# First MLP product of a two-layer decoder trunk: token operand's high and low part streamed as one 512-column product

## Chip, cores and metric

The kernel runs on one core of one Trainium2 chip. The metric is the device time of one execution in microseconds (us), as the median of the runs. Instruction starts and durations come from one profiled execution.

## What is computed

The reference is a trunk of two layers on 256 tokens of width 2048, all in float32. The part that matters here is the MLP of each layer, with 8192 hidden columns:

```python
m = rmsnorm(h, pre_ff_norm)
y = jnp.square(jax.nn.relu(m @ w_ff1)) @ w_ff2
h = h + rmsnorm(y, post_ff_norm)
```

Ahead of it stand an input projection, sparse attention with a top-k indexer, retention and an output projection. Behind it stands a gated per-layer embedding. Every large product is made from float32 weights that are read once from device memory.

## The kernel before

**Split products.** Each float32 operand is cut into a high part (rounded to the type float32r) and a low part (what the rounding left). A product is the sum of three: high times high, high times low, low times high. TensorE thus makes three passes for each tile of 128 rows of the contraction (a K-tile, 16 of them in the width of 2048).

**Weight stream.** `prep` (L260) loads two K-tiles of 512 weight columns (a half, 512 KB) by a DMA on SP's queue into one of 3 buffers `raw`. ScalarE writes the high part `whi` (L271) and VectorE the low part `wlo` (L272), each into one of 7 buffers. A `Unit` holds two halves (four K-tiles) and its matmuls. The loop over units (L958 on) calls `prep_to` ahead of the unit's matmuls, and the unit's `after` behind them.

**Token-major products.** `a_units` (L275): the tokens are the stationary operand, 512 weight columns stream past (L291, L292, L293), and each of two token tiles has its own PSUM bank. The second MLP product `ff2` (L856) is made so, in pieces of 8 K-tiles. Its result is added into `Y` by VectorE (L867, L865 for the first piece).

**Transposed products.** `b_units` (L302) is used for the first MLP product alone: 128 weight columns are stationary and all 256 tokens stream past. For each of four column blocks `f` and each K-tile `k` of a unit it issues `whi` past the tokens' high part (L321), `whi` past their low part (L324) and `wlo` past their high part (L325), 256 columns each. Blocks `f` 0 and 1 share a bank, and so do 2 and 3, so that a chunk of 512 hidden columns takes two banks of the pool `ps_mm`. There are 2 layers of 8 pieces, with 2 chunks of 4 units in each.

**Behind a chunk.** `after` in `ff1` (L830) runs for each bank: Relu from the bank (L837) and Square into the high part of the hidden operand `fT` (L838) on ScalarE, then the same square in float32 (L840) and the low part (L841) on VectorE.

**Order.** Units go `ff1(0)`, `ff1(1)`, `ff2(0)`, `ff1(2)`, `ff2(1)` and so on to `ff2(7)`, so the hidden operand of a piece is used about a piece later. A scheduler orders each engine's instructions, and on each engine they are issued in that order.

**Buffers.** K-major operands of 2048 rows are `TSet`s (L214): four slots of the pool `H` (8 slots, 8 KB per partition each), two for high parts and two for low ones. Attention's operands, the hidden operand and half of the embedding product (`e1`, L816) come from `H` too. PSUM has 4 banks for large products (`ps_mm`) and 4 for transposes and small products (`ps_ax`).

Of the kernel before, what the change touches and what calls it, by code (L numbers as in the profile page):

```python
# [36 lines left out]
# columns of the constants: a part for retention alone, and a part that stays on chip  # L37
# [5 lines left out]
class Unit:  # L43
    """Up to four K-tiles of weights, and the matmuls that use them."""
# [12 lines left out]
def trunk(ctx: ExitStack, tc: tile.TileContext, x, p, positions, w_in, w_out, w_ff1, w_ff2, w_ple, w_ple_gate,  # L57
# [6 lines left out]
    hp = ctx.enter_context(tc.tile_pool(name="hp", bufs=8))  # L64
# [6 lines left out]
    # what the weights' split waits behind  # L71
# [53 lines left out]
    def tables():  # L125
        posf = small(NT, tag="posf", bufs=1)
        V.tensor_copy(posf, posi)
        ang = t2()[:, :NT * NROT]
        for t in range(NT):
            V.tensor_scalar(ang[:, t * NROT:(t + 1) * NROT], K[:, C_INV:C_INV + NROT], posf[:, t:t + 1], None, op0=OP.mult)  # L130
        # 2 pi in parts of 8 bits, so that a part times a count of 15 bits is exact in float32
        parts = _two_pi_parts()
        MAGIC = 1.5 * 2.0 ** 23
        BIG = MAGIC * 2.0 ** 14
        r = ang
        for _ in range(2):
            n = t2()[:, :NT * NROT]
            V.tensor_scalar(n, r, 0.15915494309189535, None, op0=OP.mult)
            hi = t2()[:, :NT * NROT]
            V.tensor_scalar(hi, n, BIG, BIG, op0=OP.add, op1=OP.subtract)  # L140
            lo = t2()[:, :NT * NROT]
            V.tensor_sub(lo, n, hi)
            V.tensor_scalar(lo, lo, MAGIC, MAGIC, op0=OP.add, op1=OP.subtract)
            for c in parts:
                for q in (hi, lo):
                    V.scalar_tensor_tensor(r, q, -c, r, op0=OP.mult, op1=OP.add)
        lim = 3.1415925
        V.tensor_scalar(r, r, lim, -lim, op0=OP.min, op1=OP.max)
        s1 = t2()[:, :NT * NROT]
        A.activation(s1, r, AF.Sin)  # L150
        V.tensor_tensor(sinT.rearrange("q t n -> q t n"), s1.rearrange("q (t n) -> q t n", t=NT),
                        K[:, None, C_SGN:C_SGN + NROT].to_broadcast([P, NT, NROT]), op=OP.mult)
        a1 = t2()[:, :NT * NROT]
        V.scalar_tensor_tensor(a1, r, -1.0, r, op0=OP.mult, op1=OP.max)
        V.tensor_scalar(a1, a1, -1.0, 1.5707963267948966, op0=OP.mult, op1=OP.add)
        A.activation(cosT.rearrange("q t n -> q (t n)"), a1, AF.Sin)

# [1 line left out]
    def root(v, n):  # L159
        """1/sqrt(v) on [P, n]: exponent guess, three Newton steps y (3 - v y^2) with the halves taken out beforehand."""  # L160
# [21 lines left out]
    class RowStat:  # L182
        """1/rms of rows from sums of squares that come in four parts; the first three are summed before the last is known."""
# [30 lines left out]
    class TSet:  # L214
        """K-major halves (hi, lo) of a [tokens, 2048] operand."""

        def __init__(self):
            self.hi = [None, None]
            self.lo = [None, None]

        def half(self, i):
            if self.hi[i] is None:
                self.hi[i] = hslot()
                self.lo[i] = hslot()
            return self.hi[i], self.lo[i]

# [3 lines left out]
    def after_first(first, m):  # L230
        """Keep m behind the matmul that opened its bank: the opening clears the whole bank's flags."""
        behind(m, first)
        return first or m

    def split_bank(ts, kt0, t, bank, gain=None):
        """bank [P, 4, 128] of K-tiles kt0.. for token tile t -> hi/lo."""
# [15 lines left out]
    def to_kmajor(ts, src, t, n, gain=None):  # L252
        """src: function col0 -> [P, 128] token-major block."""
# [6 lines left out]
    def prep(u, k):  # L260
        """K-tiles k, k+1 of the unit: load, and split into float32r parts."""
# [13 lines left out]
    def a_units(w, kts, cols, ts, after, kt_w0=0, ps=ps_mm):  # L275
        """Token-major product: psum[t] [128 tok, n] over K-tiles kts of ts; after(t, psum)."""
# [25 lines left out]
    def b_units(w, cols, ts, after):  # L302
        """Transposed product: psum [128 out cols, 256 tok], two column tiles per bank."""
        acc = []
        res = []
        for j in range(0, KT, 4):
            def mm(u, t, k0, j=j):
                if k0:
                    return
                opened = None  # L310
                if not acc:
                    acc.extend([ps_mm(), ps_mm()])
                for f in range(4):
                    o = acc[f // 2][:, (f % 2) * S:(f % 2 + 1) * S]
                    for k in range(4):
                        whi, wlo = u.halves[k // HALF]
                        ahi, alo = ts().get(j + k)
                        fc = slice(f * P, (f + 1) * P)
                        first = j + k == 0 and f % 2 == 0
                        last = j + k == KT - 1  # L320
                        m = T.matmul(o, whi[:, k % HALF, fc], ahi, start=first, stop=False, skip_group_check=True)  # L321
                        if j + k == 0:
                            opened = after_first(opened if f % 2 else None, m)
                        T.matmul(o, whi[:, k % HALF, fc], alo, start=False, stop=False, skip_group_check=True)  # L324
                        T.matmul(o, wlo[:, k % HALF, fc], ahi, start=False, stop=last, skip_group_check=True)  # L325
            fin = None
            if j + 4 >= KT:
                def fin(t):
                    for b in range(2):
                        after(b, acc[b])  # L330
# [6 lines left out]
    def soon(f, t):  # L337
        """In front of the side work, token tile 0 before 1."""
        side.insert(t, f)

# [1 line left out]
    def first_act():  # L342
        """K-major operand of a layer's input projection, from h; the norm's scale comes later."""
        st["aT"] = TSet()
# [12 lines left out]
    def rope(z, t, heads, width, kind):  # L357
        """In place on z [P, heads*width]."""
# [18 lines left out]
    def layer(l):  # L377
# [5 lines left out]
        def skew(n=2):  # L383
            """The last n units so far: first token tile first, for its successors' sake."""
# [16 lines left out]
        def load_zc():  # L401
# [4 lines left out]
            # block-diagonal pairs of retention states  # L406
            L["R"] = zc[:, Z_R:].rearrange("q (a e n) -> q a e n", a=4, e=2)

# [27 lines left out]
        def tr4(z, dst, j0, t):  # L436
            """Four [P, 128] blocks of z -> dst[:, j0:j0+4, tok], after the next unit."""
# [36 lines left out]
        def sc(t):  # L474
            # token tile 0 has 128 keys in row 2, tile 1 has 256 in row 0
            return L["score"][:, 2, 0:128] if t == 0 else L["score"][:, 0, :]

        def logits(t, hs):
            # heads of one parity: their operands lie in the same rows of the array
# [20 lines left out]
        def topk(t, rnd):  # L500
# [5 lines left out]
            if rnd == 3:  # L506
                nk = (t + 1) * P
                # not selected -> NEG, and not causal -> NEG
# [48 lines left out]
        def att_b(t, h0, n):  # L557
            """P -> P^T: [s, heads, q] per key block."""
# [8 lines left out]
            # [s, block, head, q]  # L567
            L["pt", t, h0] = pt.rearrange("q (b n) -> q b n", b=nb)

        def att_c(h0):  # L570
            """out^T [hd, heads, q] for 4 heads, both token tiles -> K-major halves."""
# [63 lines left out]
        def ret_inner(t, e):  # L635
            """Heads of parity e: decayed scores, transposed: [key, head, query]."""
# [62 lines left out]
        # first the chunk that needs the least: the rotary tables take their time  # L699
# [27 lines left out]
        def settle(t, ts, gain, step, sq):  # L727
            """Residual and next operand; both token tiles' first K-tiles come first."""
# [17 lines left out]
        def normed(src, t, n, i, ts, gain, step, eps=(EPS, EPS)):  # L746
            """Block n, the i-th to come, of a product that is normed and added to h."""
# [16 lines left out]
        def after_mix(n):  # L764
            def f(t, ps):
                if t == 0 and n == 0:
                    alloc_y()
                if t == 0 and n == 3:
                    L["mT"] = TSet()
# [3 lines left out]
        def mlp_scale():  # L773
            """The MLP runs on rows of h that are not normed: with v their mean square + eps, its result is v times too
            large, which the norm after it takes out if its eps is v^2 times larger."""
# [34 lines left out]
        def after_e(n):  # L810
            def f(t, ps):
                if n % 2 == 0 and t == 0:
                    if n == 0:
                        L["e"] = {0: sp.tile([P, NT, 2, 512], F32, name=nm("e0"), tag="zc", bufs=1)}
                    else:
                        L["e"][1] = hp.tile([P, NT, 2, 512], F32, name=nm("e1"), tag="H")  # L816
# [7 lines left out]
        NP = DFF // 1024  # L824

        def ff1(pc):
            res = []

            def after(c):
                def f(b, ps):  # L830
# [6 lines left out]
                    A.activation(u, ps, AF.Relu)  # L837
                    A.activation(hi[:, k:k + 2, :], u3, AF.Square)  # L838
                    sq = t2()
                    V.tensor_mul(sq, u, u)  # L840
                    V.tensor_sub(lo[:, k:k + 2, :], sq.rearrange("q (f n) -> q f n", f=2), hi[:, k:k + 2, :].bitcast(F32))  # L841
                return f
            for c in range(2):
                c0 = pc * 1024 + c * 512
                res += b_units(f1, (c0, c0 + 512), lambda: L["mT"], after(c))
# [113 lines left out]
    while i < len(units):  # L959
        # units of which the first token tile's products come first, or one unit  # L960
# [9 lines left out]
        if len(step) > 1:  # L970
            spare = HALVES - 2 * len(step)
            prep_to(end + spare)
            for t in range(NT):
# [7 lines left out]
                # as buffers come free, but not in the way of what was just started  # L981
# [36 lines left out]
def _constants():  # L1018
    """Tables that depend on shapes alone."""
# [50 lines left out]
```

## Time and profile before

| what | value |
|---|---|
| runs, us | 2425.32, 2423.05, 2427.38; median 2425.32 |
| profiled execution, span from first to last instruction | 2422.3 us; the profile lists no other time of that execution |
| TensorE matmuls (PE) | 2394.2 us busy, 99% of the span, 13737 |
| TensorE weight loads (PEld) | 2103.6 us, 87% |
| VectorE (DVE) | 1439.9 us, 59% |
| ScalarE (ACT) | 1171.1 us, 48% |
| granted TensorE clock, mean | 0.998 of full speed |
| moved from device memory | 439.91 MB, 182 GB/s over the span |

Matmuls are pipelined: the recorded duration of one is longer than the time until the next starts. What a stream of them costs is read from the distances of their starts, not from their durations. The queues of ScalarE and VectorE are followed in order: an instruction that waits holds all that stand behind it on that engine.

### The profile page before, as it was taken

What the parts mean: (1) busy time and instruction counts of PE and PEld (TensorE: products, weight loads), DVE (VectorE), ACT (ScalarE), POOL (GpSimd) and SP (SyncE); (2) the same over time, 40 slices, a digit from 0 to 9 for tenths busy, and PEclk for the clock granted to TensorE, in tenths of its full rate; (3) what the DMA queues carried; (4) which work ended last, traced back from release to release, by engine and by line L of the source; (5) the groups of instructions that cost most, each with busy time, mean ns of one, the idle gap of its engine ahead of it and who ended that gap; (6) DMA issues with size and microseconds to landing.
All of it is one profiled execution on the core that took longest, in us unless ns stands there. A gap on an engine that the chain in (4) does not pass through costs nothing.

```text
span 2422.3 us, 34917 instructions
## 1 busy us (share of the span) xinstructions
PE 2394.2 (99%) x13737; PEld 2103.6 (87%) x13737; DVE 1439.9 (59%) x2176; ACT 1171.1 (48%) x1598; POOL 2.1 (0%) x6
## 2 busy tenths in 40 slices
PE   8999999999999999999999999999999999999998
PEld 6888888989989989988888888899889989989886
DVE  6676756545555555557576767575455555555575
ACT  6545546544344334445475555474444344344453
POOL 0000000000000000000000000000000000000000
PEclk9999999999999999999999999999999999999999
DMA  7655465665666566565565555655665565665654
GB/s 240 181 166 154 144 199 174 189 193 186 181 191 193 184 191 190 182 202 183 184 201 175 165 148 159 203 169 186 193 191 183 184 198 183 186 195 184 200 187 135
DMA packets 235347, 444.27 MB, mean 183 GB/s; under 512 B 18528, under 2 KB 23472, under 8 KB 235184
## 3 DMA queue, kind: packets, MB, share of 16 engines
q1 hardware_dynamic: 233952, 441.24, 59.2%
q8 instruction: 107, 1.75, 0.3%
q10 hardware_dynamic: 1232, 0.82, 0.1%
q14 instruction: 56, 0.46, 0.1%
HBM read 439.91 MB, written 2.10 MB: 182 GB/s over the span
## 4 chain that ended last, share of the span: by engine, by line
PE 88%; DVE 4%; ACT 3%; DMA 3%; issue 1%; ACTq 0%; SPq 0%; DVEq 0%
PE mm L291 18%; PE mm L292 18%; PE mm L293 18%; PE mm L324 10%; PE mm L325 10%; PE mm L321 10%; DMA raw<-in_w_in 2%; DVE wlo L272 2%; ACT whi L271 1%; PE ax L484 1%; ACT t L248 1%; DVE h L722 1%; PE ax L256 0%; PE ax L537 0%; PE ax L579 0%
## 5 line engine op out<-in xcount | busy, mean ns | idle before, releaser
L272 DVE TENSOR_TENSOR wlo<-raw,whi 128x1024 fp32r<-128x1024 f32 (+1 forms) x824 | 994.2, 1217 | 841.1 <-ACT whi L271 834.4
L271 ACT ACTIVATE whi<-raw 128x1024 fp32r<-128x1024 f32 (+1 forms) x824 | 858.6, 1054 | 1067.4 <-PE mm L293 613.1
L291 PE MATMUL mm<-whi,H 128*128 128x512 f32 (+1 forms) x2240 | 875.2, 391 | 0.1
L292 PE MATMUL mm<-wlo,H 128*128 128x512 f32 (+1 forms) x2240 | 868.9, 388 | 0.4 <-DVE wlo L272 0.4
L293 PE MATMUL mm<-whi,H 128*128 128x512 f32 (+1 forms) x2240 | 868.1, 388 | 0.0
L324 PE MATMUL mm<-H,whi 128*128 128x256 f32 x2048 | 579.7, 283 | 0.7 <-DVE H L250 0.7
L321 PE MATMUL mm<-H,whi 128*128 128x256 f32 x2048 | 579.6, 283 | 0.3 <-ACT H L249 0.3
L325 PE MATMUL mm<-H,wlo 128*128 128x256 f32 x2048 | 579.5, 283 | 0.0
L291 PEld LDWEIGHTS mm<-whi,H 128*128 128x128 f32 x2240 | 420.9, 188 | 87.6 <-issue 2.7
L293 PEld LDWEIGHTS mm<-whi,H 128*128 128x128 f32 x2240 | 420.7, 188 | 85.7 <-DVE H L250 0.7
L292 PEld LDWEIGHTS mm<-wlo,H 128*128 128x128 f32 x2240 | 420.9, 188 | 83.1 <-DVE wlo L272 0.7
L324 PEld LDWEIGHTS mm<-H,whi 128*128 128x128 f32 x2048 | 393.1, 192 | 1.6 <-DVE H L250 1.1
L321 PEld LDWEIGHTS mm<-H,whi 128*128 128x128 f32 x2048 | 393.0, 192 | 1.7 <-ACT H L249 1.2
L325 PEld LDWEIGHTS mm<-H,wlo 128*128 128x128 f32 x2048 | 393.1, 192 | 0.0
L867 DVE TENSOR_TENSOR Y<-mm,Y 128x512 f32<-128x512 f32 x112 | 72.0, 683 | 3.0 <-PE mm L293 3.0
L837 ACT ACTIVATE t<-mm 128x512 f32<-128x512 f32 x64 | 37.7, 589 | 49.5 <-PE mm L325 49.5
L840 DVE TENSOR_TENSOR t<-t 128x512 f32<-128x512 f32 x64 | 44.0, 688 | 25.5 <-ACT t L837 25.5
L248 ACT ACTIVATE t<-ax,gK 128x128 f32<-128x128 f32 x160 | 46.8, 401 | 7.1 <-PE ax L256 6.7
L841 DVE TENSOR_TENSOR H<-t,H 128x512 fp32r<-128x512 f32 x64 | 44.1, 689 | 3.7 <-DVE t L840 0.5
L838 ACT ACTIVATE H<-t 128x512 fp32r<-128x512 f32 x64 | 40.1, 627 | 1.0
L250 DVE TENSOR_TENSOR H<-t,H 128x512 fp32r<-128x512 f32 x40 | 27.6, 690 | 15.7 <-ACT H L249 15.6
L256 PE MATMUL ax<-K,h 128*128 128x128 f32 x192 | 31.0, 299 | 5.7 <-DMA h<-in_x 3.6
(129 smaller groups left out, 828.5 us busy)
## 6 DMA issues: line engine op xcount, KB each, us to landing
raw<-in_w_ff SPq DMA_DIRECT2D x512, 512.0 KB, 4.0
raw<-in_w_in SPq DMA_DIRECT2D x160, 512.0 KB, 3.6
raw<-in_w_out SPq DMA_DIRECT2D x64, 512.0 KB, 4.5
raw<-in_w_ple_gate SPq DMA_DIRECT2D x64, 512.0 KB, 4.8
raw<-in_w_in SPq DMA_DIRECT2D x16, 256.0 KB, 3.1
raw<-in_w_ple SPq DMA_DIRECT2D x8, 512.0 KB, 4.7
h<-in_x SPq DMA_DIRECT2D x4, 512.0 KB, 5.7
gB<-in_post_mix_norm SPq DMA_DIRECT2D x8, 256.0 KB, 3.8
```

Source lines behind the costliest of these rows:

```text
L248: A.activation(u3[:, j, :], b3[:, j, :], AF.Copy, scale=gK[:, gain + kt0 + j:gain + kt0 + j + 1])
L271: behind(A.activation(hi[:, :, :u.n], raw[:, :, :u.n], AF.Copy), ha)
L272: behind(V.tensor_sub(lo[:, :, :u.n], raw[:, :, :u.n], hi[:, :, :u.n].bitcast(F32)), hv)
L291: T.matmul(o, ahi[:, tok], whi[:, k % HALF, :n], start=first, stop=False)
L292: T.matmul(o, ahi[:, tok], wlo[:, k % HALF, :n], start=False, stop=False)
L293: T.matmul(o, alo[:, tok], whi[:, k % HALF, :n], start=False, stop=last)
L321: m = T.matmul(o, whi[:, k % HALF, fc], ahi, start=first, stop=False, skip_group_check=True)
L324: T.matmul(o, whi[:, k % HALF, fc], alo, start=False, stop=False, skip_group_check=True)
L325: T.matmul(o, wlo[:, k % HALF, fc], ahi, start=False, stop=last, skip_group_check=True)
L840: V.tensor_mul(sq, u, u)
L841: V.tensor_sub(lo[:, k:k + 2, :], sq.rearrange("q (f n) -> q f n", f=2), hi[:, k:k + 2, :].bitcast(F32))
L867: V.tensor_add(L["Y"][:, t, sl], ps, L["Y"][:, t, sl])
```

## The change

The pair of high and low part of a K-tile becomes one moving operand of two runs of 256 columns, and the corrections get a half of the bank of their own:

- `TSet(paired=True)` takes one buffer `[128, 2, 8, 256]` for each 8 K-tiles from a new pool `xp` (tag `X`, 2 buffers of 16 KB), in which high and low parts lie side by side. The layer's input operand `aT` and the MLP's operand `mT` are paired now. `hp` has 4 slots in place of 8. `e1` comes from `X`.
- `b_units` issues two matmuls for each `f` and `k`: `whi` past both parts, 512 columns (L329), and `wlo` past the high part, 256 columns, into the bank's second half (L331). Each `f` has a bank of its own, four for a chunk; the first chunk of a piece takes the four of `ps_mm`, the second the four of `ps_ax`.
- Behind a chunk, for two banks each: ScalarE copies the second half of each bank (L845), VectorE adds the first half to it (L846), and ScalarE makes Relu (L847), Square (L848) and the high part (L849) from chip memory; VectorE makes the low part (L850). The separate square on VectorE is gone.

```diff
-    hp = ctx.enter_context(tc.tile_pool(name="hp", bufs=8))
+    hp = ctx.enter_context(tc.tile_pool(name="hp", bufs=4))
+    xp = ctx.enter_context(tc.tile_pool(name="xp", bufs=2))
...
         def half(self, i):
             if self.hi[i] is None:
-                self.hi[i] = hslot()
-                self.lo[i] = hslot()
+                if self.paired:
+                    self.both[i] = xp.tile([P, 2, 8, S], F32R, name=nm("X"), tag="X")
+                    self.hi[i], self.lo[i] = self.both[i][:, 0], self.both[i][:, 1]
+                else:
+                    self.hi[i] = hslot()
+                    self.lo[i] = hslot()
             return self.hi[i], self.lo[i]
+
+        def pair(self, kt):
+
+            return self.both[kt // 8][:, :, kt % 8, :]
...
-                opened = None
                 if not acc:
-                    acc.extend([ps_mm(), ps_mm()])
+                    acc.extend(ps() for _ in range(4))
                 for f in range(4):
-                    o = acc[f // 2][:, (f % 2) * S:(f % 2 + 1) * S]
+                    fc = slice(f * P, (f + 1) * P)
                     for k in range(4):
                         whi, wlo = u.halves[k // HALF]
-                        ahi, alo = ts().get(j + k)
-                        fc = slice(f * P, (f + 1) * P)
-                        first = j + k == 0 and f % 2 == 0
-                        last = j + k == KT - 1
-                        m = T.matmul(o, whi[:, k % HALF, fc], ahi, start=first, stop=False, skip_group_check=True)
-                        if j + k == 0:
-                            opened = after_first(opened if f % 2 else None, m)
-                        T.matmul(o, whi[:, k % HALF, fc], alo, start=False, stop=False, skip_group_check=True)
-                        T.matmul(o, wlo[:, k % HALF, fc], ahi, start=False, stop=last, skip_group_check=True)
+                        both = ts().pair(j + k)
+                        T.matmul(acc[f].rearrange("q (e n) -> q e n", e=2), whi[:, k % HALF, fc], both, start=(j + k == 0), stop=False,
+                                 skip_group_check=True)
+                        T.matmul(acc[f][:, S:], wlo[:, k % HALF, fc], both[:, 0, :], start=False, stop=(j + k == KT - 1),
+                                 skip_group_check=True)
...
-                        after(b, acc[b])
+                        after(b, acc[2 * b:2 * b + 2])
...
-                    A.activation(u, ps, AF.Relu)
-                    A.activation(hi[:, k:k + 2, :], u3, AF.Square)
-                    sq = t2()
-                    V.tensor_mul(sq, u, u)
-                    V.tensor_sub(lo[:, k:k + 2, :], sq.rearrange("q (f n) -> q f n", f=2), hi[:, k:k + 2, :].bitcast(F32))
+                    for f in range(2):
+                        A.activation(u3[:, f], ps[f][:, S:], AF.Copy)
+                        V.tensor_add(u3[:, f], ps[f][:, :S], u3[:, f])
+                    A.activation(u, u, AF.Relu)
+                    A.activation(u, u, AF.Square)
+                    A.activation(hi[:, k:k + 2, :], u3, AF.Copy)
+                    V.tensor_sub(lo[:, k:k + 2, :], u3, hi[:, k:k + 2, :].bitcast(F32))
...
-                res += b_units(f1, (c0, c0 + 512), lambda: L["mT"], after(c))
+                res += b_units(f1, (c0, c0 + 512), lambda: L["mT"], after(c), (ps_mm, ps_ax)[c])
```

Two places show how instructions move. The first is TensorE within a unit of `ff1`, before; `H_3440` and `H_3441` are high and low part of the tokens, and `mm_4222` is a bank.

```order
L321 MATMUL mm_4222<-H_3440,whi_4046 128x256
L324 MATMUL mm_4222<-H_3441,whi_4046 128x256
L325 MATMUL mm_4222<-H_3440,wlo_4047 128x256
L321 MATMUL mm_4222<-H_3440,whi_4052 128x256
L324 MATMUL mm_4222<-H_3441,whi_4052 128x256
L325 MATMUL mm_4222<-H_3440,wlo_4053 128x256
```

The same place now; `X_3441` holds both parts, and `mm_4109` and `mm_4110` are the banks of blocks 0 and 1.

```order
L329 MATMUL mm_4109<-X_3441,whi_3959 128x512
L331 MATMUL mm_4109<-X_3441,wlo_3960 128x256
L329 MATMUL mm_4109<-X_3441,whi_3965 128x512
L331 MATMUL mm_4109<-X_3441,wlo_3966 128x256
...
L329 MATMUL mm_4110<-X_3441,whi_3959 128x512
L331 MATMUL mm_4110<-X_3441,wlo_3960 128x256
```

Three matmuls of 256 columns become one of 512 and one of 256, with the same weights in the same order.

The second place is ScalarE behind the second chunk of piece 1, before: Relu and Square of two banks among the weight splits (`whi`).

```order
L271 ACTIVATE whi_4722<-raw_4720 128x1024
L837 ACTIVATE t_949_4708<-mm_4478 128x512
L838 ACTIVATE H_4452<-t_949_4708 128x512
L271 ACTIVATE whi_4728<-raw_4726 128x1024
L837 ACTIVATE t_951_4714<-mm_4479 128x512
L271 ACTIVATE whi_4760<-raw_4758 128x1024
L838 ACTIVATE H_4452<-t_951_4714 128x512
```

The same place now.

```order
L282 ACTIVATE whi_4497<-raw_4495 128x1024
L845 ACTIVATE t_947_4477<-ax_4309 128x256
L845 ACTIVATE t_947_4477<-ax_4310 128x256
L847 ACTIVATE t_947_4477<-t_947_4477 128x512
L845 ACTIVATE t_948_4486<-ax_4311 128x256
L848 ACTIVATE t_947_4477<-t_947_4477 128x512
L282 ACTIVATE whi_4503<-raw_4501 128x1024
L849 ACTIVATE H_4277<-t_947_4477 128x512
L845 ACTIVATE t_948_4486<-ax_4312 128x256
L282 ACTIVATE whi_4535<-raw_4533 128x1024
L847 ACTIVATE t_948_4486<-t_948_4486 128x512
L282 ACTIVATE whi_4541<-raw_4539 128x1024
```

Four instructions of ScalarE become ten (the last Square and the last high part follow below these rows), and three weight splits stand among them where two stood. Outside the MLP the order on every engine is the same as before, and SP's queue of loads is the same throughout.

## Rows read from the trace of the kernel before

**Rows 1.** Page: busy time by engine; TensorE's granted clock in 40 slices.

```profile
PE 2394.2 (99%) x13737; PEld 2103.6 (87%) x13737; DVE 1439.9 (59%) x2176; ACT 1171.1 (48%) x1598; POOL 2.1 (0%) x6
...
PEclk9999999999999999999999999999999999999999
```

**Rows 2.** Stretches (length, busy time and count by engine, clock, DMA share, GB/s): MLP; ff1, ff2.

```profile
439.00:1130.00 691.00, 690.94 (x4341) 627.58 (x4340) 381.52 (x406) 299.95 (x338) 0.00 (x0) 1.00 0.61 187
...
712.50:758.60 46.10, 46.10 (x385) 46.06 (x385) 22.77 (x23) 19.19 (x22) 0.00 (x0) 1.00 0.57 178
758.60:802.10 43.50, 43.50 (x194) 36.04 (x193) 25.59 (x26) 18.31 (x19) 0.00 (x0) 1.00 0.66 199
```

**Rows 3.** Groups: matmuls of ff1 (xcount, busy us, mean ns, idle before).

```profile
L324 PE MATMUL mm<-H,whi 128*128 128x256 f32 x2048 | 579.7, 283 | 0.7 <-DVE H L250 0.7
L321 PE MATMUL mm<-H,whi 128*128 128x256 f32 x2048 | 579.6, 283 | 0.3 <-ACT H L249 0.3
L325 PE MATMUL mm<-H,wlo 128*128 128x256 f32 x2048 | 579.5, 283 | 0.0
```

**Rows 4.** PE in order of time (start us, duration us): ff1 begins, ends, begins again.

```profile
712.54 0.28 PE L321 MATMUL mm<-H,whi 128*128 128x256 f32 x1
...
758.38 0.28 PE L324 MATMUL mm<-H,whi 128*128 128x256 f32 x1
758.50 0.28 PE L325 MATMUL mm<-H,wlo 128*128 128x256 f32 x1
758.62 0.40 PE L291 MATMUL mm<-whi,H 128*128 128x512 f32 x1
758.85 0.40 PE L292 MATMUL mm<-wlo,H 128*128 128x512 f32 x1
...
801.94 0.39 PE L293 MATMUL mm<-whi,H 128*128 128x512 f32 x1
802.16 0.28 PE L321 MATMUL mm<-H,whi 128*128 128x256 f32 x1
802.28 0.28 PE L324 MATMUL mm<-H,whi 128*128 128x256 f32 x1
```

**Rows 5.** Groups of all stages: work behind a chunk, and the nearest of half its width.

```profile
L837 ACT ACTIVATE t<-mm 128x512 f32<-128x512 f32 x64 | 37.7, 589 | 49.5 <-PE mm L325 49.5
L838 ACT ACTIVATE H<-t 128x512 fp32r<-128x512 f32 x64 | 40.1, 627 | 1.0
L840 DVE TENSOR_TENSOR t<-t 128x512 f32<-128x512 f32 x64 | 44.0, 688 | 25.5 <-ACT t L837 25.5
L841 DVE TENSOR_TENSOR H<-t,H 128x512 fp32r<-128x512 f32 x64 | 44.1, 689 | 3.7 <-DVE t L840 0.5
L633 ACT ACTIVATE zc<-ax 64x256 f32<-64x256 f32 x8 | 3.0, 376 | 2.3 <-PE ax L628 2.3
L498 DVE SCALAR_TENSOR_TENSOR zb<-t,iw,zb 128x256 f32<-128x256 f32 x30 | 14.4, 480 | 0.5
```

**Rows 6.** Group of ScalarE's weight split within 439 to 1130 us, and what ended its waits.

```profile
L271 ACT ACTIVATE whi<-raw 128x1024 fp32r<-128x1024 f32 x245 | 254.9, 1057 | 352.9 <-PE mm L293 179.1 <-PE mm L324 161.2 <-DMA raw<-in_w_ff 8.1
```

**Rows 7.** ScalarE, then VectorE in order of time in ff1, about the end of a chunk.

```profile
818.79 2.01 ACT L271 ACTIVATE whi<-raw 128x1024 fp32r<-128x1024 f32 x2 [3.75 <-PE mm L324]
822.51 0.60 ACT L837 ACTIVATE t<-mm 128x512 f32<-128x512 f32 x1 [1.71 <-PE mm L325]
...
826.95 0.62 ACT L838 ACTIVATE H<-t 128x512 fp32r<-128x512 f32 x1
...
819.88 2.36 DVE L272 TENSOR_TENSOR wlo<-raw,whi 128x1024 fp32r<-128x1024 f32 x2 [3.40 <-ACT whi L271]
```

**Rows 8.** Banks given back ahead of ff1: VectorE at 802 us, ScalarE at 396 us.

```profile
801.88 1.28 DVE L867 TENSOR_TENSOR Y<-mm,Y 128x512 f32<-128x512 f32 x2
...
396.56 0.66 ACT L817 ACTIVATE e<-mm 128x512 f32<-128x512 f32 x1
```

**Rows 9.** PE at the first unit of ff1 in layer 0.

```profile
395.00 0.50 PE L321 MATMUL mm<-H,whi 128*128 128x256 f32 x2 [0.17 <-ACT H L249]
395.87 0.39 PE L324 MATMUL mm<-H,whi 128*128 128x256 f32 x1 [0.37 <-DVE H L250]
```

More of the change, by code (lines that the diff above doesn't have):

```diff
@@ L214, in trunk, with __init__ @@
     class TSet:
-        def __init__(self):
+        def __init__(self, paired=False):
             self.hi = [None, None]
             self.lo = [None, None]
+            self.both = [None, None]
+            self.paired = paired
         def half(self, i):
             if self.hi[i] is None:
-                self.hi[i] = hslot()
-                self.lo[i] = hslot()
+                if self.paired:
[4 more added lines that the diff above has]
+                    self.lo[i] = hslot()
             return self.hi[i], self.lo[i]
+        def pair(self, kt):
+            return self.both[kt // 8][:, :, kt % 8, :]
         def get(self, kt):
@@ L300, in a_units, with b_units @@
         return res
-    def b_units(w, cols, ts, after):
+    def b_units(w, cols, ts, after, ps):
         acc = []
@@ L342, in first_act @@
     def first_act():
-        st["aT"] = TSet()
+        st["aT"] = TSet(paired=True)
     def act_chunk(t, n):
@@ L768, in f @@
                 if t == 0 and n == 3:
-                    L["mT"] = TSet()
+                    L["mT"] = TSet(paired=True)
                 normed(ps, t, n, n, L.get("mT"), gain_col("ff", l), 2)
@@ L815, in f @@
                     else:
-                        L["e"][1] = hp.tile([P, NT, 2, 512], F32, name=nm("e1"), tag="H")
+                        L["e"][1] = xp.tile([P, NT, 2, 512], F32, name=nm("e1"), tag="X")
                 A.activation(L["e"][n // 2][:, t, n % 2, :], ps, AF.Copy)
```

## The prediction, made before the changed kernel had run

> **What bounds the kernel now.** I read the page's busy times first. TensorE's matmuls are busy for 2394.2 of 2422.3 us, at full clock in every slice, and VectorE and ScalarE at 59% and 48% [rows 1]. So a change pays here only if it shortens TensorE's stream, and costs only if it makes that stream wait. The table of stretches says the same of the MLP alone: from 439 to 1130 us the matmuls fill 690.94 of 691.00 us, ScalarE 299.95 and VectorE 381.52 [rows 2]. There is no wait in that stretch to remove.
>
> What one matmul costs must not be read from its mean duration (283 ns in the groups of ff1, [rows 3]), because neighbours overlap. It is read from the starts. The first product, ff1, of one piece starts at 712.54 us and the second product, ff2, follows at 758.62: 46.08 us for 2 chunks x 4 units x 16 x 3 = 384 matmuls, which is 120.0 ns for each of 256 columns. From 758.62 to 802.16 stand 4 column blocks x 8 K-tiles x 2 token tiles x 3 = 192 matmuls of 512 columns: 43.54 us, 226.8 ns each [rows 4]. Twice the columns cost 106.8 ns more, so 256 columns are worth 106.8 ns and each matmul carries 13.2 ns that do not depend on its width. These 13.2 ns are what the change can save.
>
> **The change part by part.**
>
> *The products.* The change removes nothing of the columns: 3 x 256 become 512 + 256. It removes one matmul (and one weight load) in three. By the starts, three cost 360.0 ns and the pair 226.8 + 120.0 = 346.8 ns: 13.2 ns less. There are 2048 such triples [rows 3], so 2048 x 13.2 ns = 27.0 us. All of it lies on TensorE's path.
>
> *Alternating widths.* The trace has no stream in which a wide and a narrow product alternate, but each change of stage is one such step. From the last narrow product, 758.50, to the first wide, 758.62, and on to the next, 758.85, are 0.12 + 0.23 us; from the last wide, 801.94, over 802.16 to 802.28 are 0.22 + 0.12 us [rows 4]. So the pair lies between 0.34 and 0.35 us as the starts are rounded, and the gain between 20.5 and 41 us. I take 346.8 ns, the sum of the long stretches.
>
> *Two runs.* The wide product now reads its columns in two runs of 256. No row shows such an operand. Nothing more than a wide product is one end; 13.2 ns more, as if each run were a product of its own (2 x 120.0 = 240), is the other. I take nothing, since the nearest rows, 512 columns in one stream at 226.8 ns, differ in one address step. The second end is a rival below.
>
> The rule that speaks against this change is in the Trainium skill, TensorE: Matmul & The Clock Gate, section Back-to-back issue gap: a gap of N/2.4 + 2.5 ns at full clock. By it a triple would give back 2.5 ns, 5.1 us in all (an estimate from that page), and the time would be 2420. The starts here leave 13.2 ns and not 2.5, and I go by them.
>
> *Behind a chunk.* Per pair of banks ScalarE did 0.589 + 0.627 us [rows 5]. Now it does two copies of 256 columns from PSUM, 0.376 each by the nearest row (half the partitions), and three passes over 512, about 0.627 each: 2.63 us. That is 1.42 us more, 64 times: 91 us on ScalarE. VectorE did 0.688 + 0.689 and will do two sums of 256 columns, 0.480 each by the nearest row, and 0.689: 0.27 us more, 17 us in all. In the ff1 stretch of 46.10 us ScalarE was busy for 19.19 and VectorE for 22.77 [rows 2]; with four pairs of banks they come to about 25 and 24 of 44.4 us. The cover is large, so I cost this at nothing.
>
> But the queues are in order, and weight splits stand among these instructions. So the question is how late a split may come. In the MLP ScalarE's splits wait for TensorE to give a buffer back (179.1 + 161.2 us), hardly for loads (8.1 us) [rows 6]. The pair of splits at 818.79 us goes into buffers that a unit has just freed and is complete on VectorE at 819.88 + 2.36 = 822.24, 3.5 us later [rows 7]. Of the 7 buffers 5 lie ahead, which is 2.5 units of 5.76 us, 14.4 us. So the weights are ready about 10.9 us early, and about 10.4 with units of 5.55 us. The new work holds ScalarE after the last bank closes for a copy, the wait for the sum (0.48, behind at most one split of 1.22), three passes and up to three splits of 1.06: some 7 us, where it was 0.589 + 0.627 + one split, 2.3. Five us later still leaves five. The hidden operand itself is read a piece, some 44 us, later.
>
> *Banks.* The first chunk of a piece now opens all four banks of its pool, and blocks 2 and 3 take those that ff2 used last. VectorE has emptied these at 803.16, and ff1 begins at 802.16 [rows 8, 4]; block 2 begins 8 pairs later, at 804.94. That is 1.8 us of cover, enough even if one split (1.22) goes first. At a layer's first chunk ScalarE has emptied the last bank at 397.22 [rows 8], and block 2 begins 2.8 us behind 395.87 [rows 9], at 398.6. The other pool, which the second chunk takes, is idle within the MLP. I cost the banks at nothing. If a cover failed, a split's length at 16 piece starts would cost up to 20 us.
>
> *Low part first.* At a layer's first unit two narrow products ran before the wait of 0.37 us for the low part [rows 9]. Now the first product wants both parts. That moves 0.24 us behind the wait, 0.5 in both layers at most.
>
> *Buffers and loads.* The hidden operand goes into slots whose last reader, ff2 of two pieces ago, stands ahead of it on TensorE, and attention's operands follow each other in four slots with their readers long done; no engine's order changes there. Loads in ff1 rise from 178 to about 185 GB/s, under the 199 that ff2 takes without a wait [rows 2]. Nothing is charged for either.
>
> *Sum.* 27.0 saved, some tenths lost at the start of each MLP: the span goes from 2422.3 to about 2395.3. The median of the runs, 2425.3, lies 3.0 us above that span, so the forecast is **2398 us**.
>
> **The rivals.**
>
> *No gain: the fixed cost belongs to each run.* If the 13.2 ns are paid for each run of columns, the wide product takes 240 ns, the pair 360, and nothing is saved: 2425 us. For it speaks that no row has a product in two runs. Against it speaks that the starts tie 13.2 ns to a whole matmul at both widths. By the gap of the Trainium skill's page above it would end close to here as well, at 2420.
>
> *Slower: ScalarE's queue starves the weights.* Place: the end of each of the 32 chunks. Price: what a split comes too late. It decides once splits are held over 10.4 us longer than now, and the gain is gone when each chunk stalls for 27/32 = 0.84 us, so from 11.3 us on. If the new chain held them 13 us longer, the loss would be 2.6 x 32 = 83 us and the time 2398 + 83 = 2481. For it: ten instructions that hand over between two queues, with splits between. Against it: my sum of the chain is 5 us more than before, and ScalarE is left with 19 us of idle time in 44.
>
> *More gain: weight loads set the narrow pace.* In ff1 the load side is busy for 46.06 of 46.10 us, in ff2 for 36.04 of 43.50 [rows 2]. If loads and not columns set the 120 ns, a stream with a third fewer could run by its columns alone in the narrow product, 226.8 + 106.8 = 333.6 ns: 26.4 x 2048 = 54 us, 2371 us. Against it: the load for a wide product still has only a narrow one to hide behind, and so keeps its 120 ns.
>
> **How the numbers follow.** The forecast gets 0.86, no gain 0.06, slower 0.04, more gain 0.04. The likeliest case has the pair between 343 and 350 ns (half of the rounding below, since both long stretches agree, and all of it above): 34.8 and 20.5 us saved, 2390 and 2405; 3 us of stalls at piece starts make the upper end 2408. This range holds the forecast's 0.86 but for about 0.05, so about 8 in 10, and the rivals lie outside it. A measurement can tell about 0.2%, 4.9 us, from no change. Faster by more are the forecast and the larger gain, 0.90; within it no gain, 0.06; slower 0.04.
>
> **What would show it.** In the new profile, TensorE should have 2048 matmuls fewer (11689). From one L329 to the next should be about 347 ns, so that ff1 of a piece takes about 44.4 us, with ff2 unchanged at 43.5. ScalarE's busy time should rise to about 1260 us, and VectorE's to about 1457, with no wait of TensorE for `whi`, `wlo` or a bank inside the MLP. The prediction is wrong if L329 starts stand 240 ns ahead of L331 (two runs), if TensorE waits behind ScalarE's L282 or VectorE's L283 after chunk ends (queue), or if gaps stand at block 2 of a piece's first chunk (banks).

## The result, and the profile after

| | before | changed |
|---|---|---|
| median, us | 2425.86 (4 runs, 2423.05 to 2427.38) | 2410.06 (4 runs, 2407.97 to 2414.89) |
| ratio | | 0.9936, 95% interval 0.9922 to 0.9950 |
| span of the profiled execution | 2422.3 | 2406.1 (this run took 2407.97) |
| ff1 of a later piece (third to eighth of a layer), from its first to ff2's first start | 46.08 | 45.21 |
| ff2 of such a piece | 43.54 | 43.58 |

The kernel is faster by 15.8 us, where 27 were forecast; 2410.06 lies 2 us above the range. The page of the changed kernel, busy time by engine and TensorE's clock, answers to [rows 1]:

```profile
PE 2376.0 (99%) x11689; PEld 1992.3 (83%) x11689; DVE 1446.2 (60%) x2240; ACT 1248.5 (52%) x1790; POOL 2.1 (0%) x6
...
PEclk9999999999999999999999999999999999999999
```

There are 2048 matmuls fewer, as forecast. TensorE is as full as before and its clock as high, so what is missing is not in waits. The stretches of the MLP, one ff1 and one ff2 [rows 2] (the columns are the same):

```profile
439.00:1130.00 691.00, 690.27 (x3461) 583.23 (x3460) 391.46 (x444) 342.30 (x434) 0.00 (x0) 1.00 0.60 190
707.80:753.00 45.20, 45.20 (x258) 39.18 (x257) 22.69 (x26) 22.46 (x31) 0.00 (x0) 1.00 0.58 183
753.00:796.50 43.50, 43.50 (x194) 36.00 (x193) 26.08 (x27) 19.95 (x22) 0.00 (x0) 1.00 0.64 196
```

ff1 is full of matmuls and still takes 45.21 us, by the starts 707.76 and 752.97, and not 44.4. So the matmuls themselves stand further apart than forecast. TensorE in order of time, in a later piece (start, duration):

```profile
707.76 0.39 PE L329 MATMUL mm<-X,whi 128*128 128x512 f32 x1
...
720.11 0.40 PE L329 MATMUL mm<-X,whi 128*128 128x512 f32 x1
720.35 0.28 PE L331 MATMUL mm<-X,wlo 128*128 128x256 f32 x1
720.47 0.40 PE L329 MATMUL mm<-X,whi 128*128 128x512 f32 x1
720.70 0.28 PE L331 MATMUL mm<-X,wlo 128*128 128x256 f32 x1
720.82 0.40 PE L329 MATMUL mm<-X,whi 128*128 128x512 f32 x1
721.05 0.28 PE L331 MATMUL mm<-X,wlo 128*128 128x256 f32 x1
721.17 0.40 PE L329 MATMUL mm<-X,whi 128*128 128x512 f32 x1
...
752.97 0.40 PE L302 MATMUL mm<-whi,H 128*128 128x512 f32 x1
```

Three pairs, from 720.11 to 721.17, take 1.06 us: 353.3 ns each, in a pattern of 0.36, 0.35, 0.35 us (361, 349 and 350 ns by the unrounded starts) that repeats through the piece (45.21 us for 128 pairs is 353.2). But the same code also runs faster. The same view in the first two pieces of layer 0:

```profile
429.77 0.39 PE L329 MATMUL ax<-X,whi 128*128 128x512 f32 x1
...
430.46 0.39 PE L329 MATMUL ax<-X,whi 128*128 128x512 f32 x1
...
431.16 0.39 PE L329 MATMUL ax<-X,whi 128*128 128x512 f32 x1
```

Here four pairs take 431.16 - 429.77 = 1.39 us; by the unrounded starts 1.386 us, 346.5 ns each, with pairs of 343 and 350 ns in turn. That is close to the forecast's 346.8. This fast rhythm begins behind the 16 transposes that interrupt ff1 near 403 us, and holds from 404 to 486 us, where the second piece ends. It does so again in layer 1. The twelve later pieces, entered from ff2, all keep the slow rhythm from end to end.

The queues and the work behind a chunk answer to [rows 5, 6]. ScalarE's weight split between 439 and 1130 us, and the new groups in all stages:

```profile
L282 ACT ACTIVATE whi<-raw 128x1024 fp32r<-128x1024 f32 x248 | 258.1, 1056 | 303.7 <-PE mm L304 156.6 <-PE mm L329 70.4 <-PE ax L329 51.5
```

```profile
L847 ACT ACTIVATE t<-t 128x512 f32<-128x512 f32 x64 | 40.5, 632 | 31.2 <-DVE t L846 31.2
...
L846 DVE TENSOR_TENSOR t<-mm,t 128x256 f32<-128x256 f32 x64 | 26.8, 421 | 18.9 <-ACT t L845 18.9
...
L845 ACT ACTIVATE t<-mm 128x256 f32<-128x256 f32 x64 | 24.1, 380 | 17.4 <-PE mm L331 17.4
```

ScalarE's splits still wait mostly for TensorE (156.6 + 70.4 + 51.5 of 303.7 us; for loads of MLP weights 18.1, where it was 8.1), so the weights stay early. TensorE's waits in that stretch (line waited for: us in total, times, longest) are one row, a transpose behind the last ff1, so it waits for no weight and no bank there:

```profile
PE ax L267 <- DVE h L729: 0.5, 1, 0.5
```

### The profile page after: what moved, and what is told of

Same layout as the page of the kernel before. It is cut to its first block, busy times and chain, and to the rows that moved or that the text cites. A ratio compares the mean times of both kernels' runs of the same rounds, so it can differ in the third digit from the quotient of the medians.

```text
span 2406.1 us, 31073 instructions
## 1 busy us (share of the span) xinstructions
PE 2376.0 (99%) x11689; PEld 1992.3 (83%) x11689; DVE 1446.2 (60%) x2240; ACT 1248.5 (52%) x1790; POOL 2.1 (0%) x6
## 4 chain that ended last, share of the span: by engine, by line
PE 91%; DVE 4%; ACT 2%; DMA 2%; issue 1%; ACTq 0%; DVEq 0%; SPq 0%
PE mm L302 19%; PE mm L304 19%; PE mm L303 19%; PE mm L329 10%; PE ax L329 10%; PE mm L331 5%; PE ax L331 5%; DVE wlo L283 1%; DMA raw<-in_w_in 1%; PE ax L491 1%; ACT whi L282 1%; ACT t L259 1%; PE ax L267 1%; DVE h L729 0%; PE ax L544 0%
## 5 line engine op out<-in xcount | busy, mean ns | idle before, releaser
L302 PE MATMUL mm<-whi,H 128*128 128x512 f32 x1536 | 599.3, 390 | 0.2
L303 PE MATMUL mm<-wlo,H 128*128 128x512 f32 x1536 | 598.5, 390 | 0.0
L304 PE MATMUL mm<-whi,H 128*128 128x512 f32 x1536 | 598.4, 390 | 0.0
L329 PE MATMUL mm<-X,whi 128*128 128x512 f32 x1024 | 361.4, 398 | 2.1 <-DVE X L261 2.1
L329 PE MATMUL ax<-X,whi 128*128 128x512 f32 x1024 | 360.8, 397 | 0.0
L302 PEld LDWEIGHTS mm<-whi,H 128*128 128x128 f32 x1536 | 288.4, 188 | 60.7 <-ACT H L260 1.1
L304 PEld LDWEIGHTS mm<-whi,H 128*128 128x128 f32 x1536 | 288.4, 188 | 60.1 <-DVE H L261 0.4
L331 PE MATMUL mm<-X,wlo 128*128 128x256 f32 x1024 | 287.0, 280 | 0.0
L331 PE MATMUL ax<-X,wlo 128*128 128x256 f32 x1024 | 287.0, 280 | 0.0
L302 PE MATMUL mm<-whi,X 128*128 128x512 f32 (+1 forms) x704 | 275.9, 392 | 0.0
L303 PE MATMUL mm<-wlo,X 128*128 128x512 f32 (+1 forms) x704 | 270.2, 384 | 0.4 <-DVE wlo L283 0.4
L304 PE MATMUL mm<-whi,X 128*128 128x512 f32 (+1 forms) x704 | 269.9, 384 | 0.0
L329 PEld LDWEIGHTS mm<-X,whi 128*128 128x128 f32 x1024 | 192.3, 188 | 49.6 <-DVE X L261 2.9
L329 PEld LDWEIGHTS ax<-X,whi 128*128 128x128 f32 x1024 | 192.2, 188 | 46.8
L331 PEld LDWEIGHTS mm<-X,wlo 128*128 128x128 f32 x1024 | 193.3, 189 | 0.5
L331 PEld LDWEIGHTS ax<-X,wlo 128*128 128x128 f32 x1024 | 193.3, 189 | 0.0
L302 PEld LDWEIGHTS mm<-whi,X 128*128 128x128 f32 x704 | 132.3, 188 | 27.5 <-issue 2.6
L304 PEld LDWEIGHTS mm<-whi,X 128*128 128x128 f32 x704 | 132.2, 188 | 25.8 <-DVE X L261 0.3
```

The lines of the kernel that those rows point to most:

```text
L302: T.matmul(o, ahi[:, tok], whi[:, k % HALF, :n], start=first, stop=False)
L303: T.matmul(o, ahi[:, tok], wlo[:, k % HALF, :n], start=False, stop=False)
L304: T.matmul(o, alo[:, tok], whi[:, k % HALF, :n], start=False, stop=last)
L329: T.matmul(acc[f].rearrange("q (e n) -> q e n", e=2), whi[:, k % HALF, fc], both, start=(j + k == 0), stop=False, skip_group_check=True)
L331: T.matmul(acc[f][:, S:], wlo[:, k % HALF, fc], both[:, 0, :], start=False, stop=(j + k == KT - 1), skip_group_check=True)
```

## The experiments

Each kernel is the changed one with one edit. "ff1" below is the time of a later piece, from its first start to ff2's first; the twelve of a run agree within 0.02 us but in the run with wide products alone. A ratio is to the kernel before, timed beside the run: its medians there were 2423.12 us for the first three edits and the groups of four, 2427.13 for the swapped pair and 2427.14 for the rest. Where the time went was open between three theories. **Run theory:** the wide product pays for reading two runs of 256 columns. **Evacuation theory:** banks or the work behind a chunk cost TensorE something. **Rhythm theory:** alternating widths, as such, cost more than the two long streams say, by how the stream was entered.

### High and low part side by side

```diff
-                    self.both[i] = xp.tile([P, 2, 8, S], F32R, name=nm("X"), tag="X")
-                    self.hi[i], self.lo[i] = self.both[i][:, 0], self.both[i][:, 1]
+                    self.both[i] = xp.tile([P, 8, 2, S], F32R, name=nm("X"), tag="X")
+                    self.hi[i], self.lo[i] = self.both[i][:, :, 0, :], self.both[i][:, :, 1, :]
...
-            return self.both[kt // 8][:, :, kt % 8, :]
+            return self.both[kt // 8][:, kt % 8]
```

> The changed kernel with high and low part of a K-tile next to each other in chip memory, so that the wide product reads one run of 512 columns instead of two of 256. Rhythm theory (alternating wide and narrow products fall into one of two rhythms, 353 or 346.5 ns per pair, by how the stream was entered): nothing changes, most pieces at 353 ns per pair, ff1 of a piece 45.2 us, about 2410 us. Run theory (the second run of the operand costs the missing 6.5 ns): 346.8 ns everywhere, ff1 of a piece 44.4 us, about 2399 us.

Measured: 2409.15 us, ratio 0.9941 (0.9926 to 0.9955); ff1 45.21 us, from 618.22 to 663.43. Its TensorE in order of time:

```profile
720.07 0.40 PE L329 MATMUL mm<-X,whi 128*128 128x512 f32 x1
...
720.42 0.40 PE L329 MATMUL mm<-X,whi 128*128 128x512 f32 x1
720.66 0.28 PE L331 MATMUL mm<-X,wlo 128*128 128x256 f32 x1
...
721.13 0.40 PE L329 MATMUL mm<-X,whi 128*128 128x512 f32 x1
```

Again three pairs in 1.06 us. One run of 512 columns costs what two of 256 do, and the run theory falls. In layer 1 of this kernel the fast rhythm did not appear behind the 16 transposes, though the instructions there are the same as in layer 0: which rhythm an interruption leaves is not the layout's doing.

### The wide product cut in two again

```diff
-                        T.matmul(acc[f].rearrange("q (e n) -> q e n", e=2), whi[:, k % HALF, fc], both, start=(j + k == 0), stop=False,
-                                 skip_group_check=True)
+                        T.matmul(acc[f][:, :S], whi[:, k % HALF, fc], both[:, 0, :], start=(j + k == 0), stop=False, skip_group_check=True)
+                        T.matmul(acc[f][:, S:], whi[:, k % HALF, fc], both[:, 1, :], start=False, stop=False, skip_group_check=True)
```

> The changed kernel with the wide product cut back into two products of 256 columns; banks, buffers and the work behind a chunk stay as changed. If banks and the work behind a chunk cost nothing: 360 ns for three products, ff1 of a piece 46.1 us, 2424 to 2426 us, as the kernel before. If they cost TensorE something (evacuation theory): above 2430 us.

Measured: 2423.43 us beside 2423.12 for the kernel before, ratio 0.9998 (0.9989 to 1.0007); ff1 46.07 us, as before (46.08 by rounded starts, 46.07 by unrounded ones). Its TensorE:

```profile
719.81 0.28 PE L329 MATMUL mm<-X,whi 128*128 128x256 f32 x1
719.93 0.28 PE L330 MATMUL mm<-X,whi 128*128 128x256 f32 x1
720.05 0.28 PE L331 MATMUL mm<-X,wlo 128*128 128x256 f32 x1
720.17 0.28 PE L329 MATMUL mm<-X,whi 128*128 128x256 f32 x1
```

The starts are 0.12 us apart as before. Four banks, ten instructions behind a chunk, the new pools and 77 us more on ScalarE (1248.3 us in this run) cost nothing that shows. The evacuation theory falls, and all of the gain is the wide product's.

### Interruptions: one transpose ahead of a piece, or behind its first pair

The first edit puts a transpose ahead of each piece of ff1, the second puts it behind the piece's first pair. The first:

```diff
                     acc.extend(ps() for _ in range(4))
+                    if ps is ps_mm:
+                        T.transpose(ps_ax()[:, :P], ident, ident)
```

> The changed kernel with one 128-column transpose of the identity, read by nobody, on TensorE ahead of each of the 16 pieces of ff1. Rhythm theory: the stream is entered behind a transpose as in the four pieces that ran at 346.5 ns per pair, so all pieces take 44.4 us and 0.1 to 0.3 us for the transpose, 2402 to 2405 us. Run theory and evacuation theory: the pairs stay at 353 ns, and 16 transposes are added, 2411 to 2415 us.

Measured: 2408.66 us, ratio 0.9934 (0.9919 to 0.9949); ff1 45.31 us from the first start behind the transpose. Neither forecast came true as it stood. Behind ff2's wide products the transpose changed nothing: the slow rhythm, twelve times of twelve. But the second piece of each layer, where the transpose stands behind the narrow product of a stream in the slow rhythm, ran in the fast one to its end (from 441 us in layer 0). So I moved it:

```diff
                         T.matmul(acc[f][:, S:], wlo[:, k % HALF, fc], both[:, 0, :], start=False, stop=(j + k == KT - 1),
                                  skip_group_check=True)
+                        if ps is ps_mm and j + f + k == 0:
+                            T.transpose(ps_ax()[:, :P], ident, ident)
```

> The changed kernel with one 128-column transpose that nobody reads behind the first pair of each piece of ff1, so that the alternating stream is entered again behind a narrow product, as where it ran at 346.5 ns per pair in the run with one transpose. Rhythm theory: all pieces run at 346.5 ns per pair, ff1 of a piece 44.4 us and up to 0.2 us for the transpose, 2399 to 2402 us. If the rhythm hangs on something else (chance, or what ff2 leaves behind): most pieces stay at 45.2 to 45.4 us, 2409 to 2411 us.

Measured: 2401.41 us, ratio 0.9891 (0.9876 to 0.9906); ff1 44.48 us. The entry of a piece in this kernel, and the stream further on:

```profile
707.00 0.39 PE L329 MATMUL mm<-X,whi 128*128 128x512 f32 x1
707.23 0.28 PE L331 MATMUL mm<-X,wlo 128*128 128x256 f32 x1
707.34 0.27 PE L334 MATMUL ax<-K 128*128 128x128 f32 x1
707.37 0.47 PE L329 MATMUL mm<-X,whi 128*128 128x512 f32 x1
707.68 0.28 PE L331 MATMUL mm<-X,wlo 128*128 128x256 f32 x1
...
719.94 0.39 PE L329 MATMUL mm<-X,whi 128*128 128x512 f32 x1
...
720.63 0.39 PE L329 MATMUL mm<-X,whi 128*128 128x512 f32 x1
```

Two pairs take 0.69 us, and all twelve later pieces run so. One added matmul makes a piece 0.73 us shorter. In the second piece of both layers, where the stream came in the fast rhythm, the transpose left it in the slow one. So in these two runs one transpose behind a narrow product changed the rhythm four times of four within a stream, and twelve of twelve behind an entry from ff2. (A layer's first piece is no such case. There the transpose stands ahead of a wait for data and of the first pair, in the second kernel too, where the scheduler moved it to 394.35 us; the pairs were slow until the 16 transposes. Behind these they were fast in both layers of the second kernel and slow in both of the first.)

### The pair swapped

```diff
-                        T.matmul(acc[f].rearrange("q (e n) -> q e n", e=2), whi[:, k % HALF, fc], both, start=(j + k == 0), stop=False,
+                        T.matmul(acc[f][:, S:], wlo[:, k % HALF, fc], both[:, 0, :], start=(j + k == 0), stop=False,
                                  skip_group_check=True)
-                        T.matmul(acc[f][:, S:], wlo[:, k % HALF, fc], both[:, 0, :], start=False, stop=(j + k == KT - 1),
+                        T.matmul(acc[f].rearrange("q (e n) -> q e n", e=2), whi[:, k % HALF, fc], both, start=False, stop=(j + k == KT - 1),
                                  skip_group_check=True)
```

> The changed kernel with each pair swapped: the narrow product first, then the wide one; no instruction more or less. Coming from ff2's wide products, only one wide product in a row stands ahead of each narrow one, where the changed kernel has two at the entry. If it is two wide products in a row at the entry that set the slow rhythm: 346.5 ns per pair, ff1 of a piece 44.4 us, about 2399 us. If it takes an interruption (the transpose) behind the change of width to leave the slow rhythm: 353 ns, 45.2 us, about 2410 us.

Measured: 2411.15 us, ratio 0.9933 (0.9917 to 0.9950); ff1 45.22 us:

```profile
621.21 0.28 PE L329 MATMUL mm<-X,wlo 128*128 128x256 f32 x1
...
666.43 0.40 PE L302 MATMUL mm<-whi,H 128*128 128x512 f32 x1
```

All twelve later pieces keep the slow rhythm. So neither the order within the pair nor two wide products in a row at the entry sets it.

### Fewer changes of width

Four wide products, then four narrow ones, for each block and unit:

```diff
                                  skip_group_check=True)
+                    for k in range(4):
+                        whi, wlo = u.halves[k // HALF]
+                        both = ts().pair(j + k)
                         T.matmul(acc[f][:, S:], wlo[:, k % HALF, fc], both[:, 0, :], start=False, stop=(j + k == KT - 1),
```

> The changed kernel with the four wide products of a block and unit first and its four narrow ones behind them, so that widths change twice in eight products instead of eight times. Rhythm theory: 4 x 226.8 + 4 x 120.0 = 1387 ns for a block, 346.8 per pair, ff1 of a piece 44.4 us, about 2399 us. Run theory: the wide products keep the 6.5 ns each, ff1 of a piece 45.2 us, about 2410 us.

Measured: 2404.43 us, ratio 0.9916 (0.9899 to 0.9933); ff1 44.88 us, between the two theories' numbers. Merged rows of equal products (start, time until the last one's end, count):

```profile
720.31 0.63 PE L334 MATMUL mm<-X,wlo 128*128 128x256 f32 x4
720.78 1.09 PE L329 MATMUL mm<-X,whi 128*128 128x512 f32 x4
721.71 0.64 PE L334 MATMUL mm<-X,wlo 128*128 128x256 f32 x4
```

Four wide products take 0.93 us from start to start, where ff2's would take 4 x 0.2268 = 0.907, and four narrow ones 0.47 (0.480). By 44.88 us, a group of eight takes 1402 ns and not 1387. Either each change costs, or a wide product costs more in this stage; longer groups tell. All 16 wide of a unit, then its 16 narrow ones:

```diff
...
+                wide()
+                narrow()
```

> The changed kernel with all 16 wide products of a unit first and its 16 narrow ones behind them; widths change twice in 32 products. In the run with groups of four a group of eight took about 1404 ns and not 1387: 17 ns for two changes of width, or 4.4 ns for each wide product. Change theory (a change of width costs): 16 x 226.8 + 16 x 120.0 + 17 = 5566 ns for a unit, ff1 of a piece 44.5 us, about 2400 us. Width theory (a wide product costs 231 ns in this stage whatever stands beside it): ff1 of a piece 44.9 us as with groups of four, about 2404 us.

Measured: 2401.45 us, ratio 0.9892 (0.9875 to 0.9908); ff1 44.51 us, on the change theory's number. With every second unit the other way round:

```diff
...
+                for part in ((wide, narrow) if j % 8 == 0 else (narrow, wide)):
+                    part()
```

> As the groups of 16, but every second unit takes its narrow products first, so that widths change once in 32 products. Change theory: 5566 - 9 = 5557 ns for a unit, ff1 of a piece 44.45 us, about 2399 us. Width theory: 44.9 us, about 2404 us.

Measured: 2400.49 us, ratio 0.9885 (0.9866 to 0.9903); ff1 44.45 us, on the change theory's number again. Groups in the first of the two, then in the second:

```profile
725.65 2.08 PE L335 MATMUL mm<-X,wlo 128*128 128x256 f32 x16
727.56 3.82 PE L328 MATMUL ax<-X,whi 128*128 128x512 f32 x16
731.22 1.96 PE L335 MATMUL ax<-X,wlo 128*128 128x256 f32 x15
```

```profile
721.56 4.00 PE L335 MATMUL mm<-X,wlo 128*128 128x256 f32 x32
725.39 3.82 PE L328 MATMUL mm<-X,whi 128*128 128x512 f32 x16
729.04 2.20 PE L328 MATMUL ax<-X,whi 128*128 128x512 f32 x9
```

The 16 wide products take 3.66 us, 0.03 more than 16 x 0.2268. The 16 narrow ones in front take 1.91 (1.92), and 32 narrow ones 3.83 (3.84). By the single starts, the first five wide products behind a narrow one stand 228 to 236 ns apart and the later ones 226.8: a change to wide costs about 27 ns, and the first two narrow products behind a wide one give back 8. These prices give the time of a piece: 128 x (226.7 + 120.0) ns are 44.38 us; with 7 changes to wide and 8 to narrow inside a piece the first kernel comes to 44.50, and with 4 and 4 the second to 44.45 (measured 44.51 and 44.45). They do not carry over to single pairs: there two changes in full would give about 366 ns, and neither rhythm is that slow.

### Wide products alone

```diff
-                        T.matmul(acc[f].rearrange("q (e n) -> q e n", e=2), whi[:, k % HALF, fc], both, start=(j + k == 0), stop=False,
-                                 skip_group_check=True)
-                        T.matmul(acc[f][:, S:], wlo[:, k % HALF, fc], both[:, 0, :], start=False, stop=(j + k == KT - 1),
+                        T.matmul(acc[f].rearrange("q (e n) -> q e n", e=2), whi[:, k % HALF, fc], both, start=(j + k == 0), stop=(j + k == KT - 1),
                                  skip_group_check=True)
```

> The changed kernel without the narrow products (weights' low part past the tokens' high part is left out), so that ff1 is one stream of wide products. Change theory: the starts stand 226.8 ns apart, as in ff2, where loads keep up. Width theory: 231 ns or more. The stage asks for weights faster than they have been loaded so far, so waits for loads may stand between; the usual distance is what counts, not the time.

Measured: 2216.18 us in one run. Other chunks wait for banks and weights; this one, at a granted clock of 1.00, has no wait in it:

```profile
758.27 13.99 PE L329 MATMUL ax<-X,whi 128*128 128x512 f32 x61
```

From the first of 61 starts to the last are 13.99 - 0.39 = 13.60 us, 226.7 ns for each of 60 distances. The wide product costs in this stage what it costs in ff2. The width theory falls.

## Why the prediction was right or wrong

**What bounds the kernel: right.** TensorE's stream sets the time, no wait came in the place of the products that went, and the gain is the wide product's (the run with three narrow products).

**Alternating widths: the step that failed.** I took the pair at 346.8 ns, the sum of the two long streams. That price exists, in about a quarter of the pairs. In the twelve later pieces the pair costs 353.2, and 12 x 128 x 6.4 ns is 9.8 us of the 10.8 by which the span's gain of 16.2 fell short of 27.0. Two starts at each change of stage [rows 4] gave bounds of 340 to 350. The first products behind a change keep to them: in groups of 16 the first wide one took 233 ns and the first narrow one 113, 346 together, which is the fast rhythm. The slow rhythm has a third pair of 361 ns behind two of 349 and 350, and no single change of stage shows it; it takes several pairs in a row to see it. The range was drawn to 350, so that 353 lay outside it. That alternation in the slow rhythm costs the missing time is shown by the transpose behind the first pair, which gave 0.73 us per piece back. Why the stream keeps the one rhythm or the other stays open.

**The fixed cost of 13.2 ns: right for each matmul in a steady stream.** Groups of 16 in alternating order give back 46.07 - 44.45 = 1.62 us per piece, 12.7 ns per triple. The Trainium skill, TensorE: Matmul & The Clock Gate, section Back-to-back issue gap, gives 2.5 ns over the columns at full clock, as the gap of an isolated matmul. An estimate from it is 0.3 us per piece; no steady stream here agrees with it.

**Two runs: right, nothing.** Side by side or apart, 45.21 us. The sign I had named for a cost of the runs, 240 ns from L329 to L331, does stand in the slow rhythm at one pair in three (720.11 to 720.35). It stands there with a single run too (720.42 to 720.66), so it was no sign of the runs.

**Behind a chunk and banks: right at nothing.** The second chunk's pool was not idle in the MLP, as I had it (16 transposes near 403 us write to it), but no wait came of that. ScalarE came to 1248.5 us (forecast 1262) and VectorE to 1446.2 (1457): the sum of 256 columns took 421 ns, not 480, and the copy 380 (376).

**Low part first: right.** TensorE at the first unit in layer 0 of the changed kernel:

```profile
395.91 0.50 PE L329 MATMUL mm<-X,whi 128*128 128x512 f32 x1 [1.03 <-DVE X L261]
```

It waits 1.03 us for the low part, where it waited 0.17 + 0.37 [rows 9], and ff1 begins 0.9 us later. But most of that is no loss: the first product that reads the low part began at 395.87 before and begins at 395.91 now, and only the 0.24 us of work that ran ahead of it has moved behind. The last product ahead of ff1 and the first of ff2 behind the first two pieces, before and now, bear this out:

```profile
394.44 0.39 PE L293 MATMUL mm<-whi,pT 128*128 128x512 f32 x1
...
489.75 0.40 PE L291 MATMUL mm<-whi,H 128*128 128x512 f32 x1
```

```profile
394.49 0.40 PE L304 MATMUL mm<-whi,pT 128*128 128x512 f32 x1
...
486.62 0.39 PE L302 MATMUL mm<-whi,H 128*128 128x512 f32 x1
```

From one to the other are 95.31 us and then 92.13. The two pieces, mostly in the fast rhythm, gained 3.18 us, where 256 x 13.2 ns less 0.24 us is 3.14. So this term was not what the forecast lacked.

**The rivals.** No gain: fell (the two runs cost nothing). Slower: fell (TensorE waited for no weight in the MLP). More gain by loads setting the narrow pace: no stream showed it; the narrow product kept 120 ns in groups of 16.

## What to carry to other kernels

A fixed cost per matmul can be saved by making products wider, but a stream that mixes widths can cost more than the sum of its uniform streams, so group products of one width and change seldom. Price such a stream from several of its own pairs in a row: here one start at a change showed 340 to 350 ns, and the stream ran at 353. When a rhythm of starts differs between two places that run the same code, count the pairs in each before looking for a wait.

## What was not expected of the hardware

The same alternating stream of 512 and 256 columns has two steady rhythms, 346.5 and 353.3 ns per pair, at full clock and without a wait; each holds for the rest of the stream, across banks and weight buffers (82 us in the longest fast case). Coming from wide products it was always the slow one. One interruption by a 128-column transpose behind a narrow product changed it in all 16 cases where the stream was running or had been entered from ff2 one pair before. A transpose behind ff2's wide products left the slow rhythm in all 12, and behind 16 transposes either could follow. What keeps the rhythm stays open: no run here separates possible causes in the supply of instructions, of weights or of moving operands. Three versions (groups of 16, the same with alternating order, the one transpose) came to 2400 to 2401 us, faster than both kernels, and their intervals do not tell them apart.
